# A hybrid decoder layer on one core: the second half's low-rank weights in a tile of their own, loaded ahead of the half

## The chip, the cores and the metric

The kernel runs on one core of a Trainium2 chip. The metric is the device time of one execution in microseconds, as the median over several runs. The engines are named as the profile names them: PE (TensorE matmuls), PEld (its weight loads), DVE (VectorE), ACT (ScalarE), POOL (GpSimd) and SP (SyncE), whose queue issues the DMAs here.

## What is computed

One decoder layer over 4096 tokens of 1024 channels, all in float32. A conditioning vector gives shift, scale and gate; a modulated input is multiplied by one wide weight; one half of the columns goes through a chunked gating branch (group A), the other through an RWKV-7 recurrence (group B); both are multiplied by the output weight, gated, added to the input and normalised.

```
h = x * (1 + scale) + shift ;  p = h @ w_in
out_a = gmlp_branch(p[..., :N_COLS_A], ...)
# group B, after a token shift of r, k, v, gate, wd, ad:
w_raw = -softplus(-(w0 + tanh(wd) @ w_up)) - 0.5     # w_up, a_up: 64 x 512, the low-rank weights
a = sigmoid(a0 + ad @ a_up)
S_t = S_{t-1} * decay + (S_{t-1} a_t) b_t^T + v_t k_t^T ;  y_t = S_t r_t     # per head of 64
out_b = (groupnorm(y) + bonus) * silu(gate)
y = LayerNorm(alpha * x + gate * (concat(out_a, out_b) @ w_out))
```

## The kernel before

Three stages follow each other. The first computes group A, block by block of T = 256 tokens, and leaves on the way in DRAM what the later stages read again: the modulated input in two parts (`xhl`), the low-rank activations (`wds`), the gates of group B (`sgd`) and prepared weights (`wps`). The middle stage computes group B. The last stage is the output projection with the norm.

**The middle stage** takes group B in two halves of 256 channels (`ph` 0 and 1), and each half over NSB = 16 blocks of tokens. A half and a block make a *unit*: units 0 to 15 are the first half, units 16 to 31 the second. A unit has two half-units (`p` 0 and 1). For each there is a dense part (the k, r and v projections into `psd`: 144 PE matmuls in a unit, with weights `w_k`, `w_r`, `w_v`), a token shift through a buffer `pv` (tag "pv", two buffers), the rates (`pw`, the two low-rank products), a tail (`pn`, `pt`, `pA`, `pb`), an inversion of small triangular blocks (`pG`, `pY`, 32x32 matmuls) and a scan with the state `S` (`pC`, `pU`). A *unit's mark* below is the start of its first `pG` group on PE: in the order of PE's rows the n-th such group belongs to unit n.

**What sets the order.** In the middle stage the streams (scan, inversion, tail, dense, and small ones that they spawn) yield their operations one by one to `Weave` (from line 80). It keeps a clock of its own for each engine, a time at which each tile is ready, and takes at each step the operation that can start first by these clocks; the four compute engines then run in exactly that order. So each planned time bears on the order of all that follows. `Weave.load` (line 83) issues a DMA on SP's queue and books its tile as ready some two microseconds after the planner's present time. SP's queue itself is not part of the manual order: the scheduler below sets the DMAs in an order by what they wait for and when their buffers are asked for. SP's queue issues in order: a DMA that waits holds all that stand behind it.

**The low-rank weights.** `setup(ph)` (line 807) is called once in each half, at the first half-unit of units 0 and 16, by the dense stream ahead of its projections. It clears two quarters of a tile `wua` on POOL, loads `w_up` and `a_up` for its half (256 columns of 64 rows, once into each half of the partitions, so two DMAs for each of the two) into buffers named `up` of the tag "pv" (line 813), rounds each on ACT (`CAST wua<-up`) and takes the rest on POOL. The products `pw` read `wua` after unit 16's k projection (line 899).

**The block weights of the second half.** During unit 15 `load_b1()` (line 431) asks for the six weights k, r, v of both half-units, 1 MB each, in the ring of seven buffers that the first half's weights stand in. A load waits until PE is done with the weight in its buffer, and so `w_v` of the second half-unit, the last of them, waits for the last projection of unit 15. `load_out` uses the same ring for the output weights `wo` later. `reload_parts` (line 306) reloads the modulated input of each unit in four DMAs of 512 KB (`hx<-xhl`).

## Time and profile before

| what | value |
|---|---|
| median of 3 runs | 2535.2 us (2526.46 to 2551.6) |
| the profiled execution, device time | 2542.27 us |
| its span from first to last instruction | 2540.6 us |
| PE busy, PEld busy | 2392.1 us (94%), 2085.9 us (82%) |
| DVE, ACT, POOL busy | 1564.3 us (62%), 1267.4 us (50%), 769.4 us (30%) |
| mean granted PE clock | 0.980 of full speed |

The profile is of one execution of the program. Busy times are sums over an engine; a matmul's end is modelled, so that a busy PE is not PE at its peak. [...] In a timeline a row is a run of like instructions, and the bracket at its end is the idle time of its engine just before it with what ended it; "issue" there means that the engine waited for nothing that the profile shows. Line 166 is the line of `Weave` that records every operation of the middle stage, so these are told apart by tile names.

### The profile page before, as it was taken

The numbers are of one execution on the slowest core, as the hardware profiler recorded it, in microseconds if no ns is written. First come the engines' busy times: TensorE is split into PE (matmuls) and PEld (weight loads), VectorE is DVE, ScalarE is ACT, GpSimd is POOL, SyncE is SP. The second block draws the span as 40 slices with busy tenths as digits, with TensorE's granted clock in tenths as the row PEclk, the third lists the DMA queues.
The fourth block names the chain that finished last, engine by engine and source line by source line (L and its number), as shares of the span: only waits on it lengthen the run. The fifth ranks groups of instructions, "written<-read, shape, count | busy, mean of one in ns | idle before, by whom it ended". The sixth has DMA issues, their size and how long they took to land.

```text
span 2540.6 us, 57950 instructions
## 1 busy us (share of the span) xinstructions
PE 2392.1 (94%) x22676; PEld 2085.9 (82%) x22676; DVE 1564.3 (62%) x4199; ACT 1267.4 (50%) x2946; POOL 769.4 (30%) x1423
## 2 busy tenths in 40 slices
PE   6999999999999989999999989999999988899998
PEld 4788888778888888988888878888888887688887
DVE  3544444345434358778688777788776777555555
ACT  2544544444444566756666656667665555211111
POOL 3422323232222432333333323333332233222221
PEclk9999999999999999999999999999998999999999
DMA  7533444443322532232222342322212124344442
GB/s 267 195 113 121 150 158 158 154 159 108 116 71 71 174 101 76 68 89 84 60 83 59 125 143 67 89 70 75 84 56 84 56 76 154 111 144 146 149 143 98
DMA packets 182075, 286.15 MB, mean 113 GB/s; under 512 B 14500, under 2 KB 123172, under 8 KB 180008
## 3 DMA queue, kind: packets, MB, share of 16 engines
q1 hardware_dynamic: 181800, 282.44, 34.2%
q8 instruction: 178, 2.92, 0.5%
q14 instruction: 97, 0.79, 0.1%
HBM read 188.00 MB, written 94.38 MB: 111 GB/s over the span
## 4 chain that ended last, share of the span: by engine, by line
PE 55%; DVE 18%; ACT 7%; DMA 7%; issue 4%; POOL 2%; SPq 0%; DVEq 0%; ACTq 0%; POOLq 0%
PE pso L1220 13%; PE psd L166 11%; PE psd L370 8%; PE psd L371 4%; PE pU L166 3%; PE pC L166 3%; DMA gt<-gate_row 2%; PE pA L166 2%; DVE big L166 2%; DVE X L166 2%; DVE tmp L166 2%; DVE S L166 1%; DMA wps_o<-whi 1%; PE pY L166 1%; DMA hst<-in_xT_dram 1%
## 5 line engine op out<-in xcount | busy, mean ns | idle before, releaser
L1220 PE MATMUL pso<-wo,hx 128*128 128x512 f32 x1440 | 330.5, 391 | 1.7 <-POOL hx L1220 1.2
L1220 PEld LDWEIGHTS pso<-wo,hx 128*128 128x128 f32 x1440 | 270.3, 188 | 60.6 <-POOL hx L1220 1.7
L166 PE MATMUL psd<-hx,w_v 128*128 128x256 f32 x1512 | 251.0, 293 | 13.0 <-DVE kt L166 5.5
L166 PE MATMUL psd<-hx,w_r 128*128 128x256 f32 x1512 | 250.6, 291 | 3.3 <-issue 1.9
L166 PE MATMUL psd<-hx,w_k 128*128 128x256 f32 x1512 | 239.9, 299 | 4.8 <-DVE rt L166 4.8
L166 PEld LDWEIGHTS psd<-hx,w_v 128*128 128x128 f32 x1512 | 204.7, 192 | 19.1 <-DVE kt L166 7.0
L381 DVE TENSOR_TENSOR sum<-psd,sum 128x256 f32<-128x256 f32 x208 | 87.4, 422 | 207.8 <-ACT sum L380 207.7
L166 PEld LDWEIGHTS psd<-hx,w_k 128*128 128x128 f32 x1512 | 204.1, 199 | 7.5 <-DVE rt L166 6.0
L166 PEld LDWEIGHTS psd<-hx,w_r 128*128 128x128 f32 x1512 | 204.5, 191 | 6.7 <-issue 2.1
L370 PE MATMUL psd<-hx,w_u 128*128 128x512 f32 x512 | 189.5, 412 | 8.4 <-POOL hx L259 8.2
L370 PE MATMUL psd<-hx,w_gb 128*128 128x512 f32 x512 | 185.5, 403 | 8.4 <-ACT vg L601 7.3
L370 PE MATMUL psd<-hx,w_g 128*128 128x512 f32 x512 | 181.7, 398 | 0.0
L371 PE MATMUL psd<-hx,w_u 128*128 128x256 f32 x512 | 146.2, 286 | 4.2 <-POOL w_u L259 4.2
L1220 POOL TENSOR_TENSOR hx<-hst,hx 128x512 fp32r<-128x512 f32 x58 | 82.9, 1432 | 220.5 <-ACT hx L1220 216.2
L371 PE MATMUL psd<-hx,w_gb 128*128 128x256 f32 x512 | 145.4, 284 | 0.0
L371 PE MATMUL psd<-hx,w_g 128*128 128x256 f32 x512 | 143.7, 281 | 0.0
L166 ACT ACTIVATE pv<-psd,V 128x256 f32<-128x256 f32 x192 | 89.9, 474 | 101.1 <-PE psd L166 97.7
L166 POOL COPY halo<-pv 128x1 f32<-128x1 f32 x192 | 40.2, 210 | 318.6 <-ACT pv L166 313.0
L1220 DVE SCALAR_TENSOR_TENSOR z<-z,pso 128x512 f32<-128x512 f32 x60 | 41.2, 687 | 146.9 <-PE pso L1220 146.9
L370 PEld LDWEIGHTS psd<-hx,w_u 128*128 128x128 f32 x512 | 98.6, 193 | 38.5 <-POOL hx L259 14.5
L370 PEld LDWEIGHTS psd<-hx,w_gb 128*128 128x128 f32 x512 | 97.6, 191 | 35.9 <-ACT vg L601 8.6
L380 ACT COPY sum<-psd 128x256 f32<-128x256 f32 x208 | 75.8, 365 | 93.4 <-PE psd L371 92.7
(222 smaller groups left out, 5879.7 us busy)
## 6 DMA issues: line engine op xcount, KB each, us to landing
hx<-xhl SPq DMA_DIRECT2D x126, 512.0 KB, 3.9
xhl<-hx SPq DMA_DIRECT2D x64, 512.0 KB, 2.8
hst<-in_xT_dram SPq DMA_DIRECT2D x64, 256.0 KB, 3.0
hst<-oT SPq DMA_DIRECT2D x64, 256.0 KB, 2.8
z<-in_x_dram SPq DMA_DIRECT2D x32, 512.0 KB, 3.5
out_dram<-z SPq DMA_DIRECT2D x32, 512.0 KB, 3.0
wst<-in_w_in_dram SPq DMA_DIRECT2D x42, 256.0 KB, 3.5
wa<-in_w_ada_dram SPq DMA_DIRECT2D x8, 1024.0 KB, 11.2
```

What stands on the lines that cost most here:

```text
L166: fn(*a, **k)
L370: pe.matmul(ps, w[:, 0, k], both, start=(k == 0), stop=(k == KD - 1), skip_group_check=True)
L371: pe.matmul(ps[:, 0], w[:, 1, k], both[:, 0], start=False, stop=(k == KD - 1), skip_group_check=True)
L380: s.copy(t_, ps[:, 1])
L381: v.tensor_tensor(t_, ps[:, 0], t_, op=ALU.add)
L1220: fn(*a, **k)
```

## The change

A function `fetch_low(ph)` loads both low-rank weights of a half into one tile `up` of a tag of its own, with one buffer. It is called at the first half-unit of unit 0 (for half 0, directly ahead of `setup`) and at that of unit 15 (for half 1, ahead of the block weights). `setup` then reads the tile instead of loading. Nothing else is changed: the same eight DMAs, the same ACT and POOL operations, 2 KB more in each partition, and the buffers "pv" serve the token shift alone.

```diff
+        def fetch_low(ph):
+            up = W.tile(tp, [P, 2, 256], F32, "up", 1)
+            for q, src in enumerate((w_up, a_up)):
+                for r in range(2):
+                    W.load(up[64 * r:64 * r + 64, q], src[:, ph * 256:(ph + 1) * 256])
+            R["up", ph] = up
+
         def setup(ph):
 
             wua = W.tile(tp, [P, 4, 256], F32R, "wua", 1)
             yield gp.memset(wua[:, 2:4].bitcast(F32), 0.0)
-            for q, src in enumerate((w_up, a_up)):
+            for q in range(2):
                 r_ = slice(64 * q, 64 * q + 64)
-                up = W.tile(tp, [P, 257], F32, "pv", 2, "up")[:, 0:256]
-                for r in range(2):
-                    W.load(up[64 * r:64 * r + 64], src[:, ph * 256:(ph + 1) * 256])
+                up = R["up", ph][:, q]
                 yield ac.copy(wua[:, q], up)
                 yield gp.tensor_tensor(wua[r_, 2 + q], up[r_], wua[r_, q].bitcast(F32), op=ALU.subtract)
             R[ph] = wua
@@ dense(hs) @@
             if p == 0:
+
+                if u in (0, NSB - 1):
+                    fetch_low((u + 1) // NSB)
                 if ph not in R:
                     yield from setup(ph)
```

**SP's queue at the end of unit 15.** Before, the four loads of the second half's `up` stand behind the last block weight (`w_v_18130`, from `wps_105`) and ahead of the next unit's input:

```order
L428 DMA w_r_18126<-wps_r_103 128x2048
L316 DMA hx<-xhl_146 128x1024 x3
L428 DMA w_v_18130<-wps_v_105 128x2048
L84 DMA up<-in_w_up_dram 64x256 x2
L84 DMA up<-in_a_up_dram 64x256 x2
L316 DMA hx<-xhl_147 128x1024
L1174 DMA oT_175<-yo 128x2x128
```

In the changed kernel they stand at the very start of the middle stage, since their buffer comes free there: behind the first half's four loads and the first unit's `wd` and `sgt`, and ahead of `wd` of unit 1.

```order
L84 DMA up<-in_w_up_dram 64x256 x2
L84 DMA up<-in_a_up_dram 64x256 x2
L84 DMA wd<-wds_130 128x512
L84 DMA sgt<-sgd_114 128x2x128
L84 DMA up<-in_w_up_dram 64x256 x2
L84 DMA up<-in_a_up_dram 64x256 x2
L84 DMA wd<-wds_131 128x512
L316 DMA hx<-xhl_147 128x1024
```

So the loads moved not by a unit but by fifteen, past all of the first half's DMAs; behind `w_v` the next input now follows directly.

**PE at the start of unit 16.** `pC<-S` and `pU<-rhs` are steps of the scan of unit 14, `psd<-hx,w_k_17626` is the first projection of unit 16, `pw` the low-rank products. Before:

```order
L166 MATMUL pC<-S_8614,AR 128x128 x2
L166 MATMUL pU<-rhs_8615,yt_8619 128x128 x2
L166 MATMUL psd<-hx,w_k_17626 128x256 x9
L166 MATMUL pU<-UV,BT 128x128 x2
L166 MATMUL psd<-hx,w_k_17626 128x256 x12
L166 MATMUL pt_18262<-K,BK 128x128 x4
L166 MATMUL pC<-S_8614,AR 128x128 x2
L166 MATMUL psd<-hx,w_k_17626 128x256 x3
L166 MATMUL pw<-wd,wua 128x256 x4
```

Now:

```order
L166 MATMUL pC<-S_8614,AR 128x128 x2
L166 MATMUL psd<-hx,w_k_17630 128x256 x9
L166 MATMUL pU<-rhs_8615,yt_8619 128x128 x2
L166 MATMUL psd<-hx,w_k_17630 128x256 x12
L166 MATMUL pU<-UV,BT 128x128 x2
L166 MATMUL psd<-hx,w_k_17630 128x256 x3
L166 MATMUL pt_18262<-K,BK 128x128 x4
L166 MATMUL pw<-wd,wua 128x256 x8
```

The planner no longer holds the projections back until its booked landing of `up`, and nine of them stand ahead of the scan's `pU`. Ahead of this place the order of the whole first half is the same as before, but for a few rows in units 0 and 1; from here to the end of the middle stage the planner's order is another one on all engines.

**PE at unit 20.** The rows from the mark of unit 20 on in the kernel before (`pG_21888` is the inversion's second step):

```order
L166 MATMUL pG<-xd,am 32x32 x32
L166 MATMUL pU<-UV,BT 128x128 x2
L166 MATMUL pt_21747<-K,BK 128x128 x4
L166 MATMUL pY<-yl,G 32x16 x32
L166 MATMUL pC<-UV,am 64x64 x8
L166 MATMUL pA<-AR,BK 128x128 x8
L166 MATMUL psd<-hx,w_r_18126 128x256 x3
```

The same place in the changed kernel:

```order
L166 MATMUL pG<-xd,am 32x32 x32
L166 MATMUL pA<-AR,BK 128x128 x8
L166 MATMUL pC<-UV,am 64x64 x8
L166 MATMUL pY<-yl,G 32x16 x32
L166 MATMUL pb<-hlr,onesr 128x256 x2
L166 MATMUL psd<-hx,w_r_18130 128x256 x3
L166 MATMUL psd<-hx,w_v_18134 128x256 x3
L166 MATMUL pT<-K,ysb 128x128 x2
```

And the rows from the mark of unit 3 on, in the first half of the kernel before:

```order
L166 MATMUL pG<-xd,am 32x32 x32
L166 MATMUL pA<-AR,BK 128x128 x8
L166 MATMUL pC<-UV,am 64x64 x8
L166 MATMUL pY<-yl,G 32x16 x32
L166 MATMUL pb<-hlr,onesr 128x256 x2
L166 MATMUL psd<-hx,w_r_8431 128x256 x3
L166 MATMUL psd<-hx,w_v_8468 128x256 x3
L166 MATMUL pT<-K,ysb 128x128 x2
```

But for buffer numbers the last two are the same, and they stay the same for 624 rows: from the mark of unit 20 to that of unit 30 the changed kernel has on PE, DVE and ACT, row for row, the order that units 3 to 12 have. In the kernel before, units 24 to 29 repeat one and the same order of rows, which stands nowhere in the first half.

## Rows read from the trace of the kernel before

**Rows 1.** The page: two lines of its busy times, instruction queue among DMA queues

```profile
PE 2392.1 (94%) x22676; PEld 2085.9 (82%) x22676; DVE 1564.3 (62%) x4199; ACT 1267.4 (50%) x2946; POOL 769.4 (30%) x1423
...
q8 instruction: 178, 2.92, 0.5%
```

**Rows 2.** Stretches between unit marks: length, busy by engine, PE clock, DMA share

```profile
core 0: us, PE busy (x) PEld busy (x) DVE busy (x) ACT busy (x) POOL busy (x), PEclk, DMA share, GB/s
1049.41:1437.67 388.26, 366.66 (x5132) 337.27 (x5131) 306.31 (x875) 252.41 (x633) 126.67 (x304) 1.00 0.26 76
1473.39:1517.94 44.55, 37.32 (x510) 34.25 (x509) 30.45 (x87) 26.01 (x67) 15.63 (x37) 0.92 0.38 119
1517.94:1714.15 196.21, 184.40 (x2571) 170.88 (x2571) 155.35 (x439) 125.56 (x313) 61.50 (x147) 0.99 0.26 78
1714.15:2128.60 414.45, 385.50 (x5138) 354.37 (x5137) 309.40 (x876) 251.30 (x632) 132.27 (x304) 0.94 0.25 78
1869.21:2128.60 259.39, 237.85 (x3077) 218.46 (x3073) 184.15 (x524) 151.36 (x378) 77.55 (x180) 0.91 0.25 80
2128.60:2540.60 412.00, 388.92 (x2218) 317.15 (x2214) 227.79 (x350) 81.12 (x202) 103.81 (x93) 0.99 0.40 134
```

**Rows 3.** Timeline at the change of halves: start, duration, engine, instruction, idle before

```profile
1480.13 0.32 SPq L428 DMA_DIRECT2D w_v<-wps_v  x1
...
1481.54 1.12 SPq L84 DMA_DIRECT2D up<-in_w_up_dram  x2
...
1486.26 0.41 ACT L166 CAST wua<-up 128x256 fp32r<-128x256 f32 x1 [3.40 <-DMA up<-in_w_up_dram]
...
1488.53 1.23 PE L166 MATMUL pU<-rhs,yt 128*128 128x128 f32 x4 [3.61 <-ACT rhs L166]
...
1489.41 2.19 PE L166 MATMUL psd<-hx,w_k 128*128 128x256 f32 x9
...
1491.44 0.61 PE L166 MATMUL pU<-UV,BT 128*128 128x128 f32 x4
1491.80 1.67 PE L166 MATMUL psd<-hx,w_k 128*128 128x256 f32 x12
```

**Rows 4.** Tile up, both halves: time from issue to landing of its DMAs

```profile
DMA to landing us min/median/max: 2.2/3.0/4.1
```

**Rows 5.** PE's waits, units 24 to 29: total us, times, longest

```profile
PE pA L166 <- issue: 8.3, 4, 2.4
PE psd L166 <- issue: 5.0, 2, 3.1
PE psd L166 <- DVE kt L166: 4.1, 6, 0.7
```

**Rows 6.** DMA queues in units 24 to 29: packets, MB, share

```profile
q8 instruction: 24, 0.39, 0.6%
```

**Rows 7.** PE's timeline: the burst and wait in unit 27, and in unit 9

```profile
1997.99 0.75 PE L166 MATMUL pG<-xd,am 32*32 32x32 f32 x64
...
2003.00 0.90 PE L166 MATMUL pA<-AR,BK 64*128 64x128 f32 x6 [1.80 <-issue]
...
1294.68 0.45 PE L166 MATMUL pC<-UV,am 128*64 128x64 f32 x6 [0.38 <-issue]
```

**Rows 8.** Stretches around such bursts in units 27 (two), 9, 4 and 11

```profile
1994.46:2003.00 8.54, 6.74 (x185) 6.03 (x185) 6.18 (x22) 4.15 (x12) 2.25 (x5) 1.00 0.69 217
2003.00:2013.50 10.50, 10.50 (x114) 9.36 (x114) 4.72 (x10) 4.66 (x12) 1.80 (x5) 0.52 0.18 51
1288.00:1295.00 7.00, 6.54 (x178) 5.85 (x177) 6.70 (x17) 5.81 (x16) 2.76 (x6) 1.00 0.12 40
1086.00:1091.00 5.00, 4.40 (x93) 3.85 (x93) 4.96 (x12) 3.42 (x9) 1.99 (x7) 1.00 0.42 137
1357.00:1362.00 5.00, 4.73 (x109) 4.28 (x108) 4.92 (x15) 1.60 (x5) 2.95 (x5) 1.00 0.50 144
```

**Rows 9.** Timeline at the start of the middle stage

```profile
893.76 0.40 ACT L166 CAST wua<-up 128x256 fp32r<-128x256 f32 x1 [7.79 <-DMA up<-in_w_up_dram]
...
896.96 2.07 PE L166 MATMUL pw<-wd,wua 128*128 128x256 f32 x8 [5.32 <-DVE kt L166]
```

## The prediction

> **What bounds the kernel now.** I read the page first. PE is busy for 94% of the span, DVE for 62% and the others for less [rows 1], so a gain must come out of PE's idle time or out of stretches in which PE ran at its lower clock. Then I cut the middle stage at the unit marks (the starts of PE's first `pG` group of each unit) and read length, busy time and granted clock of the stretches [rows 2]. The reader is to see that the stage does not run at one pace. Units 3 to 12 take 388.26 us, that is 38.8 us a unit, at a clock of 1.00. Units 24 to 29 take 259.39 us, 43.2 us a unit, at 0.91. Both do the same work. Units 15 to 19 take 39.2 us each, and unit 14, in which the halves change, 44.55 us. Third, I read the timeline at the change of halves [rows 3], which is where the diff acts, and last PE's waits in units 24 to 29 [rows 5], since the change moves the planner's order there too.

> At the change of halves the chain is plain. SP issues the last block weight at 1480.13 and the first `up` behind it at 1481.54; ACT stands from 1482.86 to 1486.26 for it (3.40 us), and with it all that is behind the cast on ACT: the norm of k, the exponentials, and the copy `rhs`. PE waits 3.61 us for that copy [rows 3].

> **What the change does, part by part.**

> *The wait at the half.* The cast's input now lands some fifteen units earlier. The cast (0.41 us) stays and nothing waits for it. What it delayed starts 3.4 us earlier. PE also ran slowly behind the wait: its 4 `pU` took 1.23 us where the next 4 took 0.61, and 9 projections took 2.19 us where 12 then took 1.67, so 9 cost 1.25. That is 0.6 + 0.9 = 1.5 us, and the granted clock of this unit is 0.92 [rows 2, 3]. Price: 3.6 + 1.5 = **5 us** gained. What is late next is `rhs` itself, behind the four ACT steps of 0.4 us each, about 1.7 us; nine projections (1.25 us), which now stand ahead of `pU`, cover most of it. If a wait for the last k, r, v shifts of unit 15 took the place, 1 us would remain; I keep 1 to 5.

> *The moved loads.* Eight DMAs before, eight now, of 64 KB each. The four moved ones land within 2.2 to 4.1 us [rows 4] at the start of the stage; on SP they wait for POOL's second subtraction. Behind them stands `wd` of unit 1, which waits for `pw` of unit 0 (896.96 to 899.0) anyway, so nothing there is late. PE waits 5.32 us at this place for the chain load, cast, subtraction, shift [rows 9]; the loads, ACT's casts and POOL's subtractions stand there as before, so this wait stays: 0, bounded by 1 us either way since a few rows move in units 0 and 1. Behind `w_v`, SP is free two to three microseconds earlier, for an input needed a unit later: 0.

> *The buffers.* The shift's two "pv" buffers no longer serve `up`; two uses in the stage: 0.

> *The new order.* This is the large term, and no line of the diff shows it. From unit 15 on all engines have another order. Units 20 to 29 get row for row the order of units 3 to 12. The trace of before has run this order, in 388.26 us. The order that it replaces took 414.45 us [rows 2]. Taken as it stands the difference is **26.2 us** gained.

> *What this difference consists of.* In units 24 to 29 PE has six waits that the profile puts down to nothing, one in each unit, 13.3 us in all; the next longest is 4.1 us for six [rows 5]. In units 3 to 12 there is none of 0.5 us. Behind each of them the clock falls: 0.52 for 10.5 us behind the wait that ends at 2003.00 [rows 7, 8]. The excess is 6 x (43.2 - 38.8) = 26.4 us, so a microsecond of such waits costs 2.0 us.

> What PE waits for there I read from the count. The queue of instructions moves 178 packets of 16.4 KB for 45,352 matmuls and weight loads [rows 1], 255 for a packet; 24 packets for six units [rows 6], four a unit. Counting PE's instructions through the trace, all six waits stand at the same place in a block of 256, 192 behind its start. So PE has run out of fetched instructions. The 32x32 matmuls empty a block fast: `pG` issues 64 with their loads, half a block, in 0.75 us [rows 7]. Whether a wait follows depends on two things: whether that place falls just behind such a burst, and whether the 512 KB input loads are moving then. In unit 27 the DMA share was 0.69 ahead of the wait of 1.80 us; in unit 9 the same place fell behind a burst too, with the share at 0.12, and the wait was 0.38 us [rows 7, 8].

> [...]

> *What the count does to units 20 to 29.* The rows are those of units 3 to 12 but they do not stand at the same place in the blocks: by my count the mark of unit 20 now stands 100 instructions further on in its block than the mark of unit 3 did. Moving the block ends by 100 through the trace of units 3 to 12, I find three bursts in which PE gets in under 4 us from the place at which the packet for a block starts at the earliest to the place at which it is needed, 288 instructions on: units 4, 11 and 12, now 21, 28 and 29. In the first two input loads move at that moment (DMA share 0.42 and 0.50 [rows 8]), and the third is alike. I estimate waits of 2.0, 2.1 and 1.2 us from the waits of units 24 to 29 (13.3 / 6 = 2.2 us at bursts that are a little shorter): 5.3 us, at 2.0 us each 10.6. Price: **10 us** lost of the 26, bounds 0 and 5 x 4.4 = 22 (a full wait in every second unit).

> *Units 15 to 19.* Their order is new; no unit of before has it. At the pace of units 3 to 12 they would take 5 x 38.8 = 194 us against 196.2 now [rows 2]. By the count three of the five have a burst near a block's end; at half a chance each of 2.2 us, at 2.0, that adds 6. Price: 2 to 4 us lost, bounds -7 and +11. I take **3**.

> *From unit 30 to the end.* 412 us, PE busy for 389 of them [rows 2]; the same matmuls in a slightly other order: 0, bounds -4 and +4.

> **The sum.** -5 - 26 + 10 + 3 = **-18 us**, made against the profiled execution: 2542.3 - 18 = 2524, a ratio of 0.993. The profiled execution lies 7 us above the median of the runs. On the median, 2535.2 x 0.993 gives **2517 us**.

> **The rivals.**

> *No fetch waits in the new order.* Units 20 to 29 run as 3 to 12 did. For it: the same rows ran without a wait; the waits need a load at the wrong moment. Against it: the count is shifted, and even unit 9, with hardly a load moving, waited 0.38 us at that place [rows 7]. Time: -5 - 26 - 2 = -33, 2502 us on the median. Faster by 1.3%.

> *Only the wait at the half.* The new order gets as many fetch waits as the old: six or seven in units 15 to 29. Then the whole is -5 us or less, 2530. For it: a unit has the same four blocks and the same bursts in any order.

> *Slower.* A fetch wait in nearly every unit from 15 to 29: 14 x 4.4 = 62 us against 26 now, less 5: +31, 2566 us. It decides from about 8 such units on (7 x 4.4 = 31 equals the 26 of now and the 5 of the half). For it: units 24 to 29 show that an order can lock to the blocks. Against: an irregular order such as that of units 3 to 12 moves about against the blocks from unit to unit, where the repeated one drifts by few instructions.

> *The change does not act* (the cast waits as before): excluded for the half, since its load stands fifteen units ahead.

> **How the numbers follow.** Forecast (a part of the gain given back) 0.52; no fetch waits 0.28; only the half 0.15; slower 0.05. A percent, 25 us, is about what a measurement of this kernel can tell from no change, since its own runs differ by 25 us. The first rival is over 1% faster for most of its width (0.25) and the forecast for its lower end (0.08): faster 0.33. Slower by over 1%: 0.04. Within 1%: 0.63. The range takes in most of the first rival and the second: 2500 to 2539.

> **What would show it.** No wait at the first cast of `wua` in unit 14's stretch, which falls from 44.6 to about 39.5 us: the first step. The stretch from the mark of unit 20 to that of unit 30: 388 says no fetch waits, 399 my forecast, over 410 the second rival; PE waits put down to "issue" in units 21, 28 and 29 and a lower clock behind them say that the count is right. If those units show no such wait, or others do, the account of the fetch is wrong, whatever the time is.

## The result, and the profile of the changed kernel

The changed kernel takes 2523.28 us (median of 20 runs, 2517.79 to 2528.49), the kernel before beside it 2534.82 us. The ratio is 0.9941, with a 95% interval of 0.9928 to 0.9954. The two medians differ by 11.5 us, the ratio stands for some 15, and the same pair measured again (e11 below) for 14: a gain of 11 to 15 us that is clear of noise and below one per cent. One of the 20 runs of the kernel before took 5937.65 us; the others lie between 2522.92 and 2551.6 us, with a median of 2534.45. The profiled execution of the changed kernel has a span of 2522.3 us, 18.3 less than that of the kernel before. Since that execution of before lay some 7 us above its median, the 18 stand for about 11 in the medians.

The page of the changed kernel has the same work and the same number of instruction packets as before [rows 1].

```profile
PE 2383.9 (95%) x22676; PEld 2076.9 (82%) x22676; DVE 1555.4 (62%) x4199; ACT 1267.4 (50%) x2946; POOL 760.9 (30%) x1423
...
q8 instruction: 178, 2.92, 0.5%
```

The stretches between unit marks, as in [rows 2]: units 3 to 12, unit 14, units 15 to 19, units 20 to 29, and from unit 30 to the end (length, busy time and number of each engine, granted clock, DMA share, GB/s).

```profile
1053.26:1441.22 387.96, 366.95 (x5132) 337.64 (x5131) 306.04 (x875) 252.16 (x633) 126.42 (x304) 1.00 0.26 77
1476.86:1519.56 42.70, 39.59 (x543) 36.87 (x542) 31.85 (x94) 26.65 (x68) 16.26 (x37) 0.96 0.39 124
1519.56:1719.10 199.54, 187.00 (x2549) 171.24 (x2545) 149.69 (x434) 126.20 (x313) 59.46 (x147) 0.97 0.25 75
1719.10:2108.80 389.70, 368.50 (x5132) 338.94 (x5131) 306.35 (x875) 251.99 (x633) 125.65 (x304) 0.99 0.27 83
...
2108.80:2522.30 413.50, 391.17 (x2211) 318.95 (x2211) 227.31 (x348) 80.65 (x200) 102.97 (x93) 0.97 0.40 134
```

Against before: up to the mark of unit 3 +3.85 us, units 3 to 12 -0.30, unit 13 -0.08, unit 14 -1.85, units 15 to 19 +3.33, **units 20 to 29 -24.75**, from unit 30 on +1.50. That is -18.3. More than the whole gain stands where no line of the diff acts.

PE's waits in units 20 to 29 (total us, times, longest), which answer to [rows 5]: the waits put down to "issue" (15.2 us in these units before) are down to one of 0.4.

```profile
PE pU L166 <- DVE UV L166: 5.1, 10, 1.2
PE psd L166 <- DVE rt L166: 3.2, 3, 1.5
PE pC L166 <- DVE S L166: 2.1, 5, 0.7
...
PE pC L166 <- issue: 0.4, 1, 0.4
```

At the change of halves (start, duration, engine, instruction, idle before; compare [rows 3]) ACT's casts no longer wait for a DMA, and PE goes from `pC` straight into nine projections:

```profile
1486.34 0.40 ACT L166 CAST wua<-up 128x256 fp32r<-128x256 f32 x1
1486.59 0.44 PE L166 MATMUL pt<-K,vt 128*128 128x128 f32 x2 [1.38 <-DVE vt L166]
...
1487.57 1.13 PE L166 MATMUL pC<-S,AR 128*128 128x128 f32 x4
1488.20 0.39 ACT L166 CAST wua<-up 128x256 fp32r<-128x256 f32 x1
1488.35 2.27 PE L166 MATMUL psd<-hx,w_k 128*128 128x256 f32 x9
```

The 3.6 us of idle time are gone. But the nine projections took 2.27 us, where nine took 1.32 us in another execution of the same kernel at a clock of 1.00 (e11 below): the clock fell here all the same, to 0.50 from 1487.7 to 1491.1 us. The records of the granted clock (`PEclk`, a share of full speed) are all at 1.00 or at 0.50, the 28 of this execution and the 36 of before's; a mean between the two is a mix of such stretches.

### The profile page after: what moved, and what is told of

Same layout as the page of the kernel before. It is cut to its first block, busy times and chain, and to the rows that moved or that the text cites. A ratio compares the mean times of both kernels' runs of the same rounds, so it can differ in the third digit from the quotient of the medians.

```text
span 2522.3 us, 57921 instructions
## 1 busy us (share of the span) xinstructions
PE 2383.9 (95%) x22676; PEld 2076.9 (82%) x22676; DVE 1555.4 (62%) x4199; ACT 1267.4 (50%) x2946; POOL 760.9 (30%) x1423
## 4 chain that ended last, share of the span: by engine, by line
PE 48%; DVE 21%; ACT 9%; DMA 8%; issue 5%; POOL 2%; SPq 0%; DVEq 0%; ACTq 0%; POOLq 0%
PE pso L1228 13%; PE psd L166 10%; PE psd L370 7%; PE psd L371 3%; PE pU L166 3%; PE pC L166 2%; DMA gt<-gate_row 2%; DVE big L166 2%; PE pA L166 2%; DVE X L166 2%; DMA hst<-in_xT_dram 2%; DVE tmp L166 2%; DVE S L166 2%; DMA wps_o<-whi 1%; ACT sa L166 1%
## 5 line engine op out<-in xcount | busy, mean ns | idle before, releaser
L166 PE MATMUL psd<-hx,w_k 128*128 128x256 f32 x1512 | 232.8, 294 | 8.9 <-DVE rt L166 7.8
L166 PEld LDWEIGHTS psd<-hx,w_k 128*128 128x128 f32 x1512 | 197.2, 193 | 13.1 <-DVE rt L166 9.7
L166 POOL COPY halo<-pv 128x1 f32<-128x1 f32 x192 | 39.5, 206 | 302.4 <-ACT pv L166 292.7
## 6 DMA issues: line engine op xcount, KB each, us to landing
wa<-in_w_ada_dram SPq DMA_DIRECT2D x8, 1024.0 KB, 10.2
```

The lines of the kernel that those rows point to most:

```text
L166: fn(*a, **k)
```

## The experiments

A block is 256 PE instructions, which come as one packet of 16 KB: the 45,352 matmuls and weight loads and the 236 semaphore instructions on PE's queue make 256.1 for each of the 178 packets [rows 1]. A burst is a run of small matmuls (`pG`, `pY`, `pA`, `pC`) that uses up a block fast: the 288 instructions up to the places of the waits in units 24 to 29 of before took 2.8 to 3.6 us, the same stretch of the other blocks there 12 to 16. A dummy is a matmul that nothing reads.

Theories: (1) the gain is the new order, because its blocks of 256 PE instructions end at other places, so that the fetch of the next block is in time (1a), and the fetch is late where input loads move (1b); (2) the gain is the early load; (3) the old order is slow by its own dependences, whatever the blocks. The lengths come from the windows between unit marks of each kernel's profiled execution, the issue waits are the sums of those that PE's waits list in units 20 to 29, and the ratio is to the kernel before on the same chip.

| kernel | median us | ratio, 95% interval | unit 14 | 15 to 19 | 20 to 29 | clock there | issue waits there |
|---|---|---|---|---|---|---|---|
| before | 2534.8 | 1 | 44.55 | 196.21 | 414.45 | 0.94 | 15.2 |
| changed | 2523.3 | 0.9941, 0.9928 to 0.9954 | 42.70 | 199.54 | 389.70 | 0.99 | 0.4 |
| e1 early load, old order | 2532.2 | 0.9987, 0.9969 to 1.0005 | 42.88 | 196.91 | 404.84 | 0.97 | 14.9 |
| e2 late load, new order | 2524.7 | 0.9958, 0.9940 to 0.9977 | 47.25 | 196.86 | 388.49 | 1.00 | 0.8 |
| e3 before + 192 instructions | 2515.9 | 0.9921, 0.9904 to 0.9938 | 46.11 | 196.66 | 383.64 | 1.00 | 5.1 |
| e4 before + 64 | 2520.4 | 0.9932, 0.9914 to 0.9950 | 46.37 | 200.58 | 382.60 | 1.00 | 3.3 |
| e5 early load, old order + 176 | 2513.4 | 0.9887, 0.9862 to 0.9911 | 41.59 | 196.28 | 388.18 | 0.99 | 4.3 |
| e6 changed + 208 | 2518.7 | 0.9911, 0.9890 to 0.9933 | 42.71 | 198.03 | 388.61 | 1.00 | 1.1 |
| e7 changed + 32 | 2526.6 | 0.9942, 0.9921 to 0.9962 | 42.68 | 199.49 | 390.23 | 1.00 | 1.6 |
| e8 before, half loads | 2515.6 | 0.9906, 0.9884 to 0.9929 | 45.55 | 199.47 | 381.59 | 1.00 | 2.6 |
| e9 before + 256 | 2535.4 | 0.9996, 0.9978 to 1.0015 | 46.19 | 197.16 | 393.59 | 0.99 | 9.3 |
| e10 early load, old order, two shifts | 2506.6 | 0.9885, 0.9867 to 0.9903 | 42.86 | 196.69 | 380.23 | 1.00 | 0.5 |
| e11 changed, again | 2522.0 | 0.9943, 0.9926 to 0.9961 | 41.27 | 196.75 | 388.32 | 1.00 | 0.9 |

Before's median was 2535.5 us beside e1 to e4, 2539.8 beside e5 to e8 and 2536.2 beside e9 to e11.

### Load and order apart: e1 and e2

e1 loads early, in units 0 and 15, as the changed kernel does, into tiles of their own (first line), but books in `setup` for the planner what the kernel before booked:

```diff
+                up = tp.tile([P, 256], F32, tag=f"up{q}", name="up", bufs=1)
...
+                up = R["up", ph][q]
+                ring = W.rings.setdefault((id(tp), "pv"), [])
+                ring.append(up.tensor.name)
+                if len(ring) > 2:
+                    W.after[up.tensor.name] = ring[-3]
+                W.ready[up.tensor.name] = W.now + 2000.0 + 64 * 256 * 0.02, None
```

> The low-rank weights are loaded a unit early into tiles of their own, as in the changed kernel, but the planner is told the same buffers and due times as before, so PE, DVE, ACT and POOL issue exactly the order of the kernel before. Theory 1 (the gain of the change is its new instruction order in units 20 to 29): only the wait for `up` at the half goes, so 1 to 5 us under the kernel before; units 20 to 29 stay near 414 us, each of units 24 to 29 near 43.2 us with issue waits of some 2 to 3 us each. Theory 2 (the gain is the early load itself): 11 to 18 us under the kernel before, units 20 to 29 near 390 us.

Measured: 3.3 us under the kernel before, with an interval that takes in no change. Units 20 to 29 took 404.84 us where I had expected some 414 (units 24 to 29 251.46, so 41.9 each), with 14.9 us of issue waits. Theory 2 falls.

PE's waits in units 24 to 29 of e1:

```profile
PE pA L166 <- issue: 7.5, 4, 2.7
PE psd L166 <- issue: 5.1, 2, 3.7
PE psd L166 <- DVE kt L166: 4.1, 6, 0.7
```

e2 is the reverse:

```diff
+            t0 = W.now
...
-                up = W.tile(tp, [P, 257], F32, "pv", 2, "up")[:, 0:256]
+                up = tp.tile([P, 257], F32, tag="pv", name="up", bufs=2)[:, 0:256]
                 for r in range(2):
-                    W.load(up[64 * r:64 * r + 64], src[:, ph * 256:(ph + 1) * 256])
+                    ld(up[64 * r:64 * r + 64], src[:, ph * 256:(ph + 1) * 256])
+                W.ready[up.tensor.name] = 0.0 if ph else t0 + 2000.0 + 64 * 256 * 0.02, None
```

> The reverse: the weights are loaded late, through the shared pv buffers, as in the kernel before, but the planner is given the due times of the changed kernel, so PE, DVE, ACT and POOL issue exactly the changed kernel's order. Theory 1 (order): 6 to 18 us under the kernel before; units 20 to 29 near 390 us; at the half the wait of 3 to 4 us for `up` is there again. Theory 2 (early load): within 4 us of the kernel before, units 20 to 29 near 414 us.

Measured: 10.8 us under the kernel before, units 20 to 29 at 388.49 us, and the wait for `up` is back:

```profile
1719.61:2108.10 388.49, 365.83 (x5133) 336.18 (x5132) 306.25 (x875) 252.46 (x633) 126.43 (x304) 1.00 0.27 83
...
1488.77 0.40 ACT L166 CAST wua<-up 128x256 fp32r<-128x256 f32 x1 [3.80 <-DMA up<-in_w_up_dram]
```

So the change is worth some 11 us by its order and some 3 by its load, of which the last is not told from nothing by e1's interval; the sum, 14.1, is what the changed kernel showed when it ran again (2536.2 - 2522.0 = 14.2).

### The same order, other block ends: e3, e4 and e9

The kernel before gets dummies ahead of the middle stage. Each counts as four PE instructions: the 32 matmuls 32x32 of a `pG` in the kernel's order are 64 in the trace of before [rows 7], with 64 weight loads. 48 of them are e3, 16 are e4, 64 (one whole block) are e9. The order of all else is that of before.

```diff
+        dm = ps_l.tile([P, 8, 32], F32, tag="l", name="dm", bufs=1)
+        for _ in range(48):
+            pe.matmul(dm[0:32, 0], K[0:32, 0:32], K[0:32, 0:32], start=True, stop=True)
```

> The kernel before with 48 dummy 32x32 matmuls (192 PE instructions with their weight loads) ahead of the middle stage; the order of all else is unchanged, only the places where PE's blocks of 256 instructions end move by 192. Theory 1a (the periodic units are slow because block ends meet the bursts of small matmuls and the fetch comes late): with this shift no block end of the middle stage meets a burst in which 288 instructions take under 4.5 us (15 such in the kernel before), so the issue waits of units 21 to 29 go, units 20 to 29 take 386 to 393 us instead of 414, and the whole is 15 to 27 us under the kernel before. Theory 3 (the old order itself is slow in these units, by its dependences): units 20 to 29 stay at 410 us or more, and the whole is within 4 us of the kernel before.

> The kernel before with 16 dummy 32x32 matmuls (64 PE instructions). Theory 1a (block ends): the block ends now meet the bursts in units 17 and 20 to 26 instead of 21 to 29, so the slow stretch moves: units 20 to 25 each 1 to 3 us slower than in the kernel before's clean repeats (over 41 us), units 27 to 29 come down from 43.2 to about 39 us each; the whole within 10 us of the kernel before. Theory 3 (order): the time of every unit stays as it was within 1 us, units 27 to 29 at 43 us.

> A control: the kernel before with 64 dummy 32x32 matmuls (256 PE instructions), a whole block, so that every block of the middle stage ends at the same instruction as in the kernel before. Theory 1a (where the blocks end): nothing changes, units 20 to 29 at 405 to 416 us with the same issue waits of 1 to 4 us in units 22 to 29, the whole within 6 us of the kernel before. If the dummies gained for another reason in the shifts by 64 and 192 (15 to 20 us), this one gains as much.

Measured: 192 more instructions make the kernel 19.6 us faster, 64 more 15.1 us, and 256 more change nothing (0.9996). Theory 3 falls, and so does every account by which the added matmuls themselves help. Units 20 to 29 took 384 and 383 us in the old order, less than in the new one (388 to 390): the old order is the better one, as soon as its block ends stand elsewhere. Units 20 to 29 of e3, PE's issue waits there, and units 20 to 29 of e9:

```profile
1717.13:2100.77 383.64, 364.97 (x5138) 335.99 (x5137) 309.00 (x876) 250.27 (x632) 132.73 (x304) 1.00 0.27 84
PE pG L166 <- issue: 5.1, 6, 1.6
...
1719.13:2112.72 393.59, 369.97 (x5137) 340.16 (x5136) 309.14 (x876) 250.66 (x632) 132.69 (x304) 0.99 0.27 82
```

e3 missed in one point: I had expected the issue waits to go. Six were left, 5.1 us in all, but the clock stayed at 1.00, and the units took 383.64 us, less than the 386 to 393 expected.

e4 missed in its detail: I had expected units 20 to 25 at over 41 us each, and they took 38.6 (1722.68 to 1954.32 us); and I had expected the whole within 10 us of the kernel before, and it came out 15.1 under it. By the count its block ends fell there into bursts (three of them as short as those of before), but the waits were three, 3.3 us in all, and the clock stayed up. Its units 26 to 29 show the repeated order with no wait for the fetch at all: 37.7 us each, at a clock of 1.00.

```profile
1954.32:2105.28 150.96, 145.42 (x2053) 134.04 (x2049) 122.11 (x350) 100.20 (x252) 51.71 (x120) 1.00 0.31 97
```

e9 missed in its units 20 to 29: 393.59 us where I had expected 405 to 416. The waits stand where they stood, but 9.3 us of them, not 15.2. Three executions with block ends at the same places (before, e1, e9) took 414, 405 and 394 us there, and the times of these kernels spread over some 20 us (2524.9 to 2545.8 for e9), those of e10, which has hardly such waits, over 6 (twelve executions of e9, five of e10).

### What makes the fetch late: e8

Half of each input's bytes, 256 KB for 512, are loaded for the units from 21 on. PE reads the high half twice, so the kernel leaves the low half of the input out of the sum:

```diff
-                ld(hl.bitcast(F32), xhl[i][:, q])
-                parts.extend((hl[:, 0, k], hl[:, 1, k]) for k in range(2))
+                if half:
+                    ld(hl[:, 0].bitcast(F32), xhl[i][:, q, 0])
+                else:
+                    ld(hl.bitcast(F32), xhl[i][:, q])
+                parts.extend((hl[:, 0, k], hl[:, 0 if half else 1, k]) for k in range(2))
...
+                    state["h"] = reload_parts((u + 1) % NSB, half=u >= 20)
```

> The kernel before, but from unit 21 on only the high half of each hx input is loaded (256 KB for 512 KB) and PE reads that half twice, so the low half of the input is left out of the sum; the order of all engines and PE's count stay the same. Theory 1b (the fetch of a PE block comes late because the input loads move then): the fetch starts 0.5 to 2 us after its request for 2.7 to 4.2, the issue waits of units 23 to 29 fall from 2.0 to 3.4 us to under 1 us each, units 24 to 29 take 38 to 41 us each for 43.2, and the whole is 10 to 25 us under the kernel before. Rival (the wait has its size whatever the loads do): units 24 to 29 stay at 42 to 43 us each.

Measured: 24.2 us faster, units 24 to 29 at 38.3 us each. PE's instructions, their order and their blocks are those of before. Setting the packets of the instruction queue against the count of PE's instructions (matmuls, weight loads and the 236 semaphore instructions on its queue), the packet that units 24 to 29 wait for started 2.7 to 4.2 us after the place in the block from which packets start at the earliest (160 of 256, 288 instructions ahead of where PE waits) in the kernel before, and 0.7 to 1.9 us in e8. The stretch of 8.54 us at the wait in unit 27, which had a DMA share of 0.69 [rows 8], has 0.44 in e8 from the same place in the order on, and PE's issue waits in units 24 to 29 went from 13.3 us [rows 5] to 2.2:

```profile
1980.34:1988.88 8.54, 8.54 (x200) 7.68 (x198) 7.48 (x25) 4.25 (x13) 2.24 (x5) 1.00 0.44 127
```

```profile
PE pA L166 <- issue: 1.4, 3, 0.6
PE psd L166 <- issue: 0.8, 1, 0.8
```

So it is the input loads that make the fetch late, and the late fetch that makes these units slow. Theory 1b stands, and its rival, a wait of one size whatever the loads do (42 to 43 us a unit), falls.

### The new order moved in its blocks: e6 and e7

The same dummies in the changed kernel, 52 of them (e6) and 8 (e7).

> The changed kernel with 52 dummy 32x32 matmuls (208 PE instructions): by its trace, only 3 block ends of the middle stage then meet a stretch in which 288 PE instructions take under 4.5 us. Theory 1a: what issue waits are left in the changed kernel (3 to 4 us in all, 1.6 of them in units 16 and 17) go, so 0 to 6 us under the changed kernel, units 20 to 29 at 386 to 390 us. If units 20 to 29 fall well under 386 us, the changed kernel still loses time to fetches that its waits don't show.

> The changed kernel with 8 dummy 32x32 matmuls (32 PE instructions): block ends meet the bursts of units 14, 19, 28 and 29. My forecast had put 2 us and a lower clock after it on each such meeting. If that size is right wherever a 512 KB load moves, the issue waits of these four places sum to 6 to 10 us and the whole is 4 to 12 us over the changed kernel; if loads of the new order rarely stand ahead of the fetch, they sum to under 3 us and the whole is within 4 us of the changed kernel.

Measured: e6 is at 0.9911, which cannot be told from the changed kernel's 0.9941 by the intervals; units 20 to 29 took 388.61 us, within what was expected. e7 is at 0.9942, no different from the changed kernel. Of its four places the first (at 1522 us, right behind the mark of unit 15) had a wait of 0.8 us by the count, that in unit 28 none, that in unit 29 about 1.5 us, within a wait that the profile puts down to DVE, and that right behind the mark of unit 20 this one:

```profile
1721.71 0.24 PE L166 MATMUL pY<-yl,G 32*32 32x16 f32 x4 [1.59 <-issue]
```

About 4 us in all, between my two bands for the waits; the time fell into the band of "no change", and the clock stayed at 1.00 in units 20 to 29. What e7 says against the forecast's price is the time, not the waits.

### A version that beats both: e5 and e10

The old order, the early load, and block ends put where they do little harm: 44 dummies ahead of the stage (e5), or 48 there and 32 more in the k block of unit 24 (e10), where nothing reads what they write.

```diff
+                if hs == 48 and group[0][0] == "k":
+                    for _ in range(32):
+                        pe.matmul(pss[0][0:32, 0:32], K[0:32, 0:32], K[0:32, 0:32], start=True, stop=True)
...
+        for _ in range(48):
+            pe.matmul(dm[0:32, 0], K[0:32, 0:32], K[0:32, 0:32], start=True, stop=True)
```

> The early load in the old order, with 44 dummy 32x32 matmuls (176 PE instructions) ahead of the middle stage. If the old order is slow only through block ends that meet bursts, it is at least as good as the new one once they don't: units 20 to 29 at 380 to 385 us (414 in the kernel before, 390 in the changed one), the stretch of unit 14 about 42 to 43 us, the whole 19 to 26 us under the kernel before and 8 to 15 us under the changed kernel. If the new order has a merit of its own, it stays above the changed kernel's time.

> The early load in the old order, with 48 dummy matmuls (192 PE instructions) ahead of the middle stage and 32 more (128) in the k block of unit 24, which runs at about 1800 us: block ends then stand as in the shift by 192 up to there, and as in the shift by 64 behind it, each where the runs showed no or few issue waits. Units 20 to 29 at 376 to 381 us; issue waits of the middle stage under 4 us in all; the whole 26 to 34 us under the kernel before, so faster than the changed kernel by 12 to 20 us.

Measured: e5 26.4 us under the kernel before, though its units 20 to 29 took 388 us for 380 to 385: 4.3 us of issue waits were left. e10 29.6 us under the kernel before and 15.4 under the changed kernel beside it; units 20 to 29 took 380.23 us, with 0.5 us of issue waits:

```profile
1708.26:2088.49 380.23, 366.70 (x5201) 337.83 (x5200) 307.81 (x876) 250.42 (x632) 131.84 (x304) 1.00 0.27 85
```

### The change of halves, and the changed kernel again: e11

> The changed kernel again, beside the version with two shifts on the same chip: 10 to 20 us under the kernel before, units 20 to 29 at 388 to 392 us.

Measured: 14.2 us under the kernel before, units 20 to 29 at 388.32 us. Its unit 14 took 41.27 us, 1.4 less than in the first profile of the same program. There PE has the same wait of 1.38 us for `vt`, but the clock does not fall behind it:

```profile
1487.63 0.44 PE L166 MATMUL pt<-K,vt 128*128 128x128 f32 x2 [1.38 <-DVE vt L166]
...
1489.07 1.32 PE L166 MATMUL psd<-hx,w_k 128*128 128x256 f32 x9
```

In e1, which has no wait for `up` either, it falls (nine projections in 2.27 us):

```profile
1483.34 0.44 PE L166 MATMUL pt<-K,vt 128*128 128x128 f32 x2 [1.39 <-DVE vt L166]
...
1484.31 1.18 PE L166 MATMUL pC<-S,AR 128*128 128x128 f32 x4
...
1486.82 2.27 PE L166 MATMUL psd<-hx,w_k 128*128 128x256 f32 x9
```

## Why the prediction was right, step by step

The time on record, 2517 us with a range of 2500 to 2539, is 6 us under the measured 2523.3; "within 1%" held. The sum of -18 us on the profiled execution met 18.3, but this agreement is in good part luck: errors cancel in it. And the prediction named a sign by which its account of the fetch would be wrong: no issue wait in units 21, 28 and 29 and no lower clock behind them. The profile lists none there (the one of 0.4 us stands at 1803.81 us, in unit 22), and the clock did not fall there. The experiments show what holds all the same (block ends: e3, e4, e9; loads: e8) and what was wrong, the size of these waits.

**The new order: right, and the largest term.** Forecast -26.2 us for units 20 to 29 at the pace of units 3 to 12; the stretch took 389.70 us, 1.7 more than its model in the same execution. e2 shows that the order alone brings it, without the early load. What the forecast did not see is that the old order is not slow: unhindered it takes 37.7 us a unit (e4), the new one 38.8 to 39.0. The new order gains because its block ends seldom make PE wait: with them at the three sets of places that were run (changed, e6, e7) units 20 to 29 took 388.3 to 390.2 us, and the old order took 380 to 414.

**The fetch waits given back in units 21, 28 and 29: mis-sized, +10 forecast, at most 2 measured.** The count of places was right: the mark of unit 20 stands where it was computed, and by the count PE gets through the 288 instructions in question in 3.0, 2.9 and 3.7 us in the three units. But the waits there were 0, 0.3 and 0.4 us. The rows of PE show it: `pY` in unit 21 runs through, and the 16 `pA` of units 28 and 29, 1.16 us long elsewhere in this trace, take 1.45 and 1.69 with the wait inside. Of the 1.7 us over the model a part is no fetch either: behind waits for ACT and DVE at 1893 us the clock was at 0.50 for 6.8 us, where at the same rows of unit 7 it was for 3.4.

```profile
1479.89 1.16 PE L166 MATMUL pA<-AR,BK 64*128 64x128 f32 x16
...
1761.38 0.73 PE L166 MATMUL pY<-yl,G 32*32 32x16 f32 x64
...
2033.62 1.45 PE L166 MATMUL pA<-AR,BK 64*128 64x128 f32 x16
...
2072.18 1.69 PE L166 MATMUL pA<-AR,BK 64*128 64x128 f32 x16
```

The step that failed reads "In the first two input loads move at that moment (DMA share 0.42 and 0.50 [rows 8]), and the third is alike", from which I took nearly the waits of units 24 to 29. The shares came out as foreseen, about a half, against 0.69 in unit 27 of before:

```profile
1757.00:1762.00 5.00, 4.36 (x169) 3.69 (x165) 4.96 (x15) 3.45 (x9) 3.38 (x10) 1.00 0.45 129
...
2027.50:2032.50 5.00, 4.76 (x109) 4.32 (x107) 4.93 (x14) 1.63 (x5) 2.96 (x5) 1.00 0.51 143
...
2065.00:2072.00 7.00, 7.00 (x188) 6.73 (x186) 6.39 (x19) 3.24 (x8) 2.03 (x4) 1.00 0.49 133
```

At such a share the packets started 0.3, 0.8 and 1.5 us after they could, for 2.7 to 4.2 in before. The means over 5 to 8 us hide the difference. From the place from which the packet starts at the earliest to its start, the DMA share was 0.31, 0.52 and 0.70 in units 21, 28 and 29 and 0.75 to 0.94 in units 24 to 29 of before; these are unit 29 of the changed kernel and unit 27 of before:

```profile
2068.68:2070.19 1.51, 1.51 (x118) 1.40 (x119) 1.51 (x4) 0.58 (x2) 0.27 (x1) 1.00 0.70 263
...
1997.99:2000.65 2.66, 2.66 (x145) 2.46 (x143) 1.86 (x11) 2.24 (x6) 0.32 (x1) 1.00 0.94 341
```

A packet then took 0.9 to 1.2 us in these nine units, and PE went on 1.2 to 1.5 us after its end; against 3 us of PE work hardly a wait is left. I had treated the load as there or not there; by these shares and e8 the delay goes with the DMA share at that moment. The factor of 2.0 per microsecond of wait, besides, is that of one execution of before; others gave 0.7 to 1.9 (below).

**The wait at the half: right in mechanism, -5 forecast, -1.85 in the two profiles.** In before SP's queue stood 6.2 us for PE's projections ahead of `w_v`, and then 1.0 us for DVE's `rt`, before it issued the first `up`. The idle 3.6 us of PE behind this load went, the clock part of 1.5 us did not. In this execution the clock fell already behind the wait for `vt`, ahead of the place. The prediction misread its rows here: in before, too, the clock was down from 1484.50 us on, behind the same wait for `vt` and ahead of the idle 3.61 us, so the slow `pU` and projections cannot all be put down to the wait for `rhs`:

```profile
1484.50:1491.30 6.80, 3.19 (x16) 2.90 (x15) 1.85 (x5) 3.21 (x9) 3.68 (x7) 0.50 0.71 193
```

How long it stays down differs: 6.8 to 10.2 us around this place in the six profiles with the late load, 0 to 6.8 in the seven with the early one. Over all profiles of the old order unit 14 took 44.6 to 46.4 us with the late load (five) and 41.6 to 42.9 with the early one (three); of the new order 47.3 (one) and 41.3 to 42.7 (four). Means differ by 3.3 and 4.9 us. Before's own execution was the fastest of its five.

**Units 15 to 19: +3 forecast, +3.33 measured.** But e2, e6, e7 and e11 have 196.9, 198.0, 199.5 and 196.8 us for the same order, so +0.5 to +3.3, with a granted clock of 1.00 in the shortest and 0.97 in the longest. The issue waits of the changed kernel there were 1.1 us in all, a third of what I had put in, so the agreement is no proof of the half chances by which I got there. For the lower bound of -7 the prediction gives no working.

**Moved loads and buffers, start of the stage: 0 forecast within 1, +3.85 measured up to unit 3.** Of this 2.33 us stand ahead of the mark of unit 0, which over the profiled runs came between 938.4 and 944.6 us; PE's wait there [rows 9] was 5.86 us for 5.32, within the bound. The other 1.5 us stand in unit 2, and not in a wait: both kernels have the same wait there, but the clock falls behind it only in the changed one. In before (first fence) 16 `pA` take 1.16 us behind it, in the changed kernel (second) 2.08:

```profile
1010.77 0.29 PE L166 MATMUL pY<-yl,G 32*32 32x16 f32 x10 [1.54 <-issue]
...
1011.63 1.16 PE L166 MATMUL pA<-AR,BK 64*128 64x128 f32 x16
```

```profile
1013.10 0.32 PE L166 MATMUL pY<-yl,G 32*32 32x16 f32 x10 [1.55 <-issue]
...
1014.50 2.08 PE L166 MATMUL pA<-AR,BK 64*128 64x128 f32 x16
```

The first part is scatter of single executions. The second is not: of the profiled runs with this wait, the three of the new order (changed, e2, e11) all have the clock at 0.50 for 3.4 us behind it and 44.6 to 45.2 us in unit 2, and the four of the old order (before, e1, e8, e9) have no such fall and 42.8 to 43.6 us, with waits of 1.3 to 1.8 us in the former and 1.0 to 1.8 in the latter. So these 1.5 us go with the new order, ahead of this place the few rows that moved in units 0 and 1, and not with the early load, which e2 does not have. How such rows would bring the clock down is not shown, and seven profiles are few. Where the block ends are shifted (e3 and e4, e6 and e7) unit 2 has neither the wait nor the fall.

**From unit 30 on: 0 within 4 forecast, +1.5 measured.** The kernels lie between 411 and 416 us there in either order.

**The rivals.** "No fetch waits in the new order" came out in the place it spoke of; its sum of 33 us did not: units 15 to 19 came out 5 us worse (+3.3 for -2), the half gave 3 less, and 5 were lost at the start and the end. "Only the wait at the half" is refuted by e1 and e2, "slower" by every run of the changed kernel.

## What to carry to other kernels

Where a kernel issues dense bursts of small matmuls, count PE's instructions (with the semaphore instructions of its queue) and see where its blocks of 256 end: a slow stretch with short waits that nothing explains, at one place of the block, may be moved by a few dummy instructions. Here 16 dummies (64 instructions) gave 0.9932, and 64 of them, a whole block, showed no cost (0.9996). Before a new order is credited for a gain (or blamed for a loss), shift the old one by less than a block and measure again: here that brought more than the change. A kernel whose times spread more than its neighbours' is worth a look for such waits: here e9, with 9.3 us of them, spread over 20.9 us, e10, with 0.5, over 5.9.
